# Letting the whole program, and not only its tails, issue in emission order on TensorE, VectorE and ScalarE

## The chip, the cores and the metric

The kernel runs on one core of one Trainium2 chip. A core has TensorE (PE in the profile: matmuls; PEld: its weight loads), VectorE (DVE), ScalarE (ACT), GpSimd (POOL) and SyncE (SP, here only issuing transfers), each with its own queue of instructions that it runs in the order in which they stand. The metric is the device time in microseconds (us) of the whole program; lower is better.

## The reference

Two layers of an encoder on 256 tokens of width 2048, float32, with sizes of all weights in the hundreds of megabytes. Each layer has an attention part and a feed-forward part, each between two norms that a conditioning vector `c` modulates:

```python
cond = jax.nn.silu(c)
for layer in range(2):
    mod = cond @ ada_w[layer] + ada_b[layer]            # 2048 x 12288
    sh1, sc1, g1, sh2, sc2, g2 = split(mod, 6)
    h = rms_norm(x, norm_g[layer, 0]) * (1 + sc1) + sh1
    y = local_dilated_mixer(...) if layer == 0 else diff_attention(...)
    x = x + g1 * rms_norm(y, norm_g[layer, 1])
    h = rms_norm(x, norm_g[layer, 2]) * (1 + sc2) + sh2
    y = conv_ffn(...)                                   # 2048 -> 2 x 5504 -> 2048, a width-3 convolution, gelu
    x = x + g2 * rms_norm(y, norm_g[layer, 3])
```

## The kernel before

All weights stream through the core once. `Plan.order` writes one sequence of 512 KB units: weight units, and between them units of the modulation matrix `ada_w` (a kernel-wide name: "modulation units"). SP fetches them in this sequence into a ring of nine tiles `raw` (`prefetch`, `load`): the next fetch is issued when the tile it writes has been used up.

A weight unit is split into a high and a low part so that TensorE multiplies at full rate and nearly full precision: ScalarE copies `raw` to `whi` (L259), VectorE subtracts to get `wlo` (L309, in `lows`), each from a ring of four. TensorE runs three products a tile (high x high, high x low, low x high): L655, L657, L658 in `feat_units` (feature-major, 256 columns) and L622 to L624 in `mm_tok` (token-major, 512). A modulation unit is multiplied by its entry of `silu(c)` and added to an accumulator `aacc` by VectorE: L280, L296 or L305 for the first of a chunk of sixteen, L284 for the others; for a few, the product is made on TensorE as rows (L272). When a chunk is complete, `ada_finish` sums `aacc` over the partitions with eight matmuls (L459; with rows also L462) and `columns` (L471, L474 on VectorE) writes the scales and shifts `mod`.

`Affine` applies them to the transposed, normalised rows (L509 on ScalarE, L511 on VectorE), `high` (L514) and `low` (L518) split the result into `hT`, which the matmuls read. The transposed rows come from `chunk_T`: scale on ScalarE (L529), four transposes on TensorE (L523), copy on ScalarE (L537). It runs eight times at the start and eight times in `late_tail`, from `Norm.keep`.

`Stream.done` is called when a weight unit's matmuls have been written: it frees the unit's place, takes up the next units as far as the split ring reaches (`advance`), runs the stages due of the chains of attention steps (`tick`), and writes the low parts. So the program emits its work already interleaved by hand. Attention 0 goes through the depth in four blocks (`GK`), and the first seven column units of feed-forward 0 in three (`FK`: k 0 to 7, 8 to 11, 12 to 15), since their modulations come late.

What stands in the queues is set in two ways. Inside `with tc.manual_schedule(engines=ORDERED)`, TensorE, VectorE and ScalarE get their instructions in the order in which the program emits them. Everywhere else a scheduler of the tile framework places them by its own model of readiness. Before the change only `tail` stood in such a block:

```python
if late_mods:
    late_tail(acc, ch, skew, run, got, evac, n0, n1)
else:
    with tc.manual_schedule(engines=ORDERED):
        tail(acc, ch, skew, run, got, evac, n0, n1, head or (lambda n: None))
```

`tail` ends feed-forward 0, attention 1 and feed-forward 1; `late_tail` ends attention 0.

Of the kernel before, what the change touches and what calls it, by code (L numbers as in the profile page):

```python
# [39 lines left out]
class Plan:  # L40
    """The order in which weight units and modulation units reach the chip."""

# [45 lines left out]
    def token_chunks(self, w, ks, late=0, lc=2, last=False):  # L88
        """512 columns at a time; of the first lc chunks, the last units come after all others"""
        pairs = [ks[i:i + 2] for i in range(0, len(ks), 2)]  # L90
        head = pairs[:len(pairs) - late]
        order = [(ch, head) for ch in range(lc)] + [(ch, pairs[len(head):]) for ch in range(lc)]
        order += [(ch, pairs) for ch in range(lc, 4)]
        for ch, ps in order:
            n = len(self.units)
            for p in ps:
                self.rows(w, p[0], len(p), ch * 512, 512)
            if last and ch == 3:
                u = len(self.units) - n
                skew = min(u, SPLIT_BUFS + HELD)  # L100
                self.held |= set(range(n + u - skew, n + u - SPLIT_BUFS))
# [49 lines left out]
    def put(self, nw, na, p=1.0):  # L151
        """nw weight units with na modulation units spread among them"""
        e = self.ia + na
        for k in range(nw):
            t = e - na + round(na * ((k + 1) / nw) ** p)
            while self.ia < t:
                self.seq.append(("a", self.ia))
                self.ia += 1
            self.seq.append(("w", self.iw))
            self.iw += 1  # L160
        while self.ia < e:
            self.seq.append(("a", self.ia))
            self.ia += 1
# [25 lines left out]
def encoder_kernel(ctx: ExitStack, tc: tile.TileContext, x, c, ada_w, ada_b, norm_g,  # L189
# [15 lines left out]
    def vy():  # L205
        return cp.tile([P, 2, D], F32, name="vy")

    plan = Plan(ab_w_in, ab_w_out, c_w_in, c_w_out, ffn_w_up, ffn_w_down)
    units, seq = plan.units, plan.seq

    class Stream:
# [100 lines left out]
        def advance(self, limit=None, lows=True, n=None):  # L312
            """use up what has been loaded, as far as the split buffers reach"""
            if n is not None:
# [36 lines left out]
        def open(self, n):  # L351
            """let n of the gated modulation units through"""
            self.gate += n
            self.advance()
# [18 lines left out]
        def chain(self, *stages, delay=0):  # L373
            """stages one tick after another, each given what the one before returned; older chains go first"""
            age = self.age = self.age + 1

            def run(k, v):
                r = stages[k](v)
                if k + 1 < len(stages):
                    self.at(1, lambda: run(k + 1, r), age)  # L380
            self.at(1 + delay, lambda: run(0, None), age)
# [14 lines left out]

# [1 line left out]
    def rows_tile():  # L398
# [37 lines left out]

# [1 line left out]
    def gate_rows(l, m):  # L438
# [36 lines left out]

# [1 line left out]
    def sums():  # L477
# [20 lines left out]
    class Affine:  # L498
        """the modulated rows of feature tiles k.. from src, split into high and low parts"""

# [33 lines left out]
    def chunk_T(t, ch, r, dst):  # L534
        """rows 4 ch.. of the normalised and transposed x"""
        z = normed(t, ch, r, tmp.tile([P, 512], F32, name="hf", bufs=3), True)
# [5 lines left out]
    class Norm:  # L542
        """x += gate * rms_norm(y), then the modulated rms_norm of x, transposed and split, for one token block"""

# [69 lines left out]

# [1 line left out]
    def mm_tok(dst, act, kt, t, hi, lo, first, last):  # L616
# [9 lines left out]
    def tok_units(dsts, act, ks, first=True, last=True, one_bank=False):  # L626
        """dsts[t] += act block t times the next weights, rows ks"""
        n = 0
        while n < len(ks):
            i, (hi, lo) = st.take()  # L630
            a = hi.shape[1]
# [7 lines left out]
    def feat_units(acc, k0, kn, n):  # L639
        """one bank: acc[:, j] += (next weights).T @ h for n // 128 feature tiles"""  # L640
        hT = cur["hT"]
# [23 lines left out]

# [1 line left out]
    def feat_out(pool, acc, scale, name, bufs=1):  # L667
# [17 lines left out]
    def probs_T(pool, parts):  # L685
        """the transposed probabilities: parts[t] lists what is summed, each with its normalising diagonal"""
        pt = bank().rearrange("p (k q) -> p k q", k=2)
# [174 lines left out]

# [1 line left out]
    def out_chunks(act, ks, evac, late=0, lc=2, norms=None, late_mods=False, head=None):  # L864
# [252 lines left out]

# [1 line left out]
    v_acc, v_got = [], []  # L1119
# [199 lines left out]
```

## Time and profile before

| what | value |
|---|---|
| device time, median of 3 runs | 2326.72 us (2321.35 to 2329.6) |
| span of the profiled execution | 2334.3 us |
| TensorE busy | 2226.5 us, 95% |
| VectorE / ScalarE / GpSimd busy | 1620.0 (69%) / 1055.0 (45%) / 45.5 us (2%) |
| transfers | 587.14 MB, mean 252 GB/s |
| mean granted TensorE clock | 0.980 |

The profiled execution has its span and no time of its own beside it; the span is 7.6 us over the median of the runs, inside 0.4%. In a profile line the idle time before an instruction stands in brackets with what ended it. The granted clock of TensorE (a share of full speed) falls to one half after a time without much work on it. A stage without loss has TensorE busy for all of its length.

The program's stages in this execution, read from the lines that run in them: start and attention 0's k-blocks up to 180 us, the rest of attention 0 to 330, `late_tail` to 370, feed-forward 0's k-blocks to 440, feed-forward 0 to 1180, attention 1 to 1600, feed-forward 1 to the end.

### The profile page before, as it was taken

Reading aid. Unit: us, or ns where it says so; the run is one execution under the profiler, and the core shown is the slowest. Engines: PE = TensorE matmul, PEld = TensorE weight load, DVE = VectorE, ACT = ScalarE, POOL = GpSimd, SP = SyncE. Lnnn points to the kernel's source line nnn. Section 1 sums busy time; section 2 is a strip of 40 time slices with the busy share of each in tenths; the row PEclk is TensorE's granted clock in tenths of the full one; section 3 lists DMA queues with packets and bytes.
Section 4 is the critical chain, followed back from the end, with each engine's and each line's share of the span. In section 5 each row is a group of like instructions: output and inputs, shape, how many; then the busy total and the mean of one; then the engine's idle time right before and its main releaser. Section 6 shows DMA issues by size and latency. Waiting matters only on the chain.

```text
span 2334.3 us, 37324 instructions
## 1 busy us (share of the span) xinstructions
PE 2226.5 (95%) x14961; PEld 2030.9 (87%) x14961; DVE 1620.0 (69%) x1802; ACT 1055.0 (45%) x1451; POOL 45.5 (2%) x72
## 2 busy tenths in 40 slices
PE   5689999999999999999999999999999999999998
PEld 3679978999877999987888999888999988999986
DVE  7888987887666677776687886657565545565555
ACT  4334455544333334434554554446444444444443
POOL 0000000000000000000000110000000000000000
PEclk8889999999999999999999999999999999999999
DMA  9999989898778888887589996665677666666652
GB/s 343 367 329 318 327 292 316 294 306 287 249 263 273 277 268 270 273 261 265 177 287 334 308 307 212 212 198 162 200 205 203 199 206 207 193 205 201 178 187 104
DMA packets 390427, 587.14 MB, mean 252 GB/s; under 512 B 18110, under 2 KB 256360, under 8 KB 389612
## 3 DMA queue, kind: packets, MB, share of 16 engines
q1 hardware_dynamic: 390252, 584.75, 77.3%
q8 instruction: 117, 1.92, 0.3%
q14 instruction: 58, 0.48, 0.1%
HBM read 582.58 MB, written 2.10 MB: 250 GB/s over the span
## 4 chain that ended last, share of the span: by engine, by line
PE 58%; DMA 17%; issue 13%; DVE 10%; ACT 1%; POOL 1%; DVEq 0%; POOLq 0%; ACTq 0%
DMA raw<-in_ada_w_dram 14%; PE bank L657 11%; PE bank L655 11%; PE bank L658 11%; PE bank L623 7%; PE bank L622 7%; PE bank L624 7%; DVE wlo L309 4%; DVE aacc L284 4%; DMA raw<-in_ffn_w_down_dram 2%; DMA raw<-in_ffn_w_up_dram 1%; PE bank L459 1%; DMA raw<-in_ab_w_in_dram 1%; PE bank L794 1%; PE bank L523 1%
## 5 line engine op out<-in xcount | busy, mean ns | idle before, releaser
L259 ACT ACTIVATE whi<-raw 128x1024 fp32r<-128x1024 f32 x708 | 740.5, 1053 | 873.9 <-PE bank L657 399.6
L309 DVE TENSOR_TENSOR wlo<-raw,whi 128x1024 fp32r<-128x1024 f32 x708 | 856.9, 1217 | 369.3 <-ACT whi L259 356.6
L658 PE MATMUL bank<-hT,wlo 128*128 128x256 f32 x3616 | 1022.7, 283 | 20.1 <-DVE wlo L309 20.0
L655 PE MATMUL bank<-hT,whi 128*128 128x256 f32 x3616 | 1027.9, 284 | 0.0
L657 PE MATMUL bank<-hT,whi 128*128 128x256 f32 x3616 | 1018.8, 282 | 0.2 <-DVE hT L518 0.2
L658 PEld LDWEIGHTS bank<-hT,wlo 128*128 128x128 f32 x3616 | 685.9, 190 | 26.8 <-DVE wlo L309 26.1
L655 PEld LDWEIGHTS bank<-hT,whi 128*128 128x128 f32 x3616 | 686.4, 190 | 3.1 <-ACT whi L259 1.0
L657 PEld LDWEIGHTS bank<-hT,whi 128*128 128x128 f32 x3616 | 686.1, 190 | 3.2 <-issue 1.7
L284 DVE SCALAR_TENSOR_TENSOR aacc<-raw,ccol,aacc 128x1024 f32<-128x1024 f32 x352 | 454.1, 1290 | 209.3 <-DMA raw<-in_ada_w_dram 207.0
L623 PE MATMUL bank<-wlo,act 128*128 128x512 f32 x656 | 261.5, 399 | 12.7 <-DVE wlo L309 12.7
L622 PE MATMUL bank<-whi,act 128*128 128x512 f32 x656 | 259.8, 396 | 0.0
L624 PE MATMUL bank<-whi,act 128*128 128x512 f32 x656 | 259.6, 396 | 0.0
L623 PEld LDWEIGHTS bank<-wlo,act 128*128 128x128 f32 x656 | 123.8, 189 | 48.6 <-DVE wlo L309 20.4
L622 PEld LDWEIGHTS bank<-whi,act 128*128 128x128 f32 x656 | 123.9, 189 | 29.0
L624 PEld LDWEIGHTS bank<-whi,act 128*128 128x128 f32 x656 | 123.9, 189 | 28.5
L622 PE MATMUL bank<-whi,hT 128*128 128x512 f32 (+1 forms) x192 | 76.0, 400 | 14.6 <-ACT hT L514 14.6
L1046 ACT ACTIVATE cv<-cv 128x512 f32<-128x512 f32 (+1 forms) x44 | 27.4, 622 | 106.0 <-DVE cv L1042 105.8
L623 PE MATMUL bank<-wlo,hT 128*128 128x512 f32 (+1 forms) x192 | 75.1, 393 | 0.0
L624 PE MATMUL bank<-whi,hT 128*128 128x512 f32 (+1 forms) x192 | 72.2, 385 | 0.0
L622 PE MATMUL bank<-whi,oT 128*128 128x512 f32 x176 | 71.0, 403 | 0.0
L623 PE MATMUL bank<-wlo,oT 128*128 128x512 f32 x176 | 69.6, 396 | 0.0
L624 PE MATMUL bank<-whi,oT 128*128 128x512 f32 x176 | 69.4, 395 | 0.0
(168 smaller groups left out, 1381.5 us busy)
## 6 DMA issues: line engine op xcount, KB each, us to landing
raw<-in_ada_w_dram SPq DMA_DIRECT2D x384, 512.0 KB, 5.3
raw<-in_ffn_w_up_dram SPq DMA_DIRECT2D x344, 512.0 KB, 4.7
raw<-in_ffn_w_down_dram SPq DMA_DIRECT2D x168, 512.0 KB, 5.2
raw<-in_c_w_in_dram SPq DMA_DIRECT2D x96, 512.0 KB, 5.3
raw<-in_ab_w_in_dram SPq DMA_DIRECT2D x56, 512.0 KB, 6.2
raw<-in_c_w_out_dram SPq DMA_DIRECT2D x32, 512.0 KB, 5.0
raw<-in_ab_w_out_dram SPq DMA_DIRECT2D x16, 512.0 KB, 5.6
gb<-in_norm_g_dram SPq DMA_DIRECT2D x3, 1024.0 KB, 4.8
```

Of the source, the lines that this page charges most:

```text
L259: nc.scalar.activation(hi, v, AF.Copy)
L284: nc.vector.scalar_tensor_tensor(self.acc, t, col, self.acc, op0=ALU.mult, op1=ALU.add)
L309: nc.vector.tensor_tensor(lo, v, hi.bitcast(F32), op=ALU.subtract)
L459: nc.tensor.matmul(t[:, j:j + 1], acc[:, j * P:(j + 1) * P], ones[:, 0:1], start=True, stop=rows is None)
L523: nc.tensor.transpose(ps[:, q * P:(q + 1) * P], src[:, q * P:(q + 1) * P], ident)
L622: nc.tensor.matmul(dst, ah, hi, start=first, stop=False, skip_group_check=True)
L623: nc.tensor.matmul(dst, ah, lo, start=False, stop=False, skip_group_check=True)
L624: nc.tensor.matmul(dst, al, hi, start=False, stop=last, skip_group_check=True)
L655: nc.tensor.matmul(acc[:, j], wh, hT[:, k, 0], start=k == 0 and j == 0, stop=False, skip_group_check=True)
L657: nc.tensor.matmul(acc[:, j], wh, hT[:, k, 1], start=False, stop=False, skip_group_check=True)
L658: nc.tensor.matmul(acc[:, j], wl, hT[:, k, 0], start=False, stop=k == KT - 1, skip_group_check=True)
L1046: nc.scalar.activation(cv[:, :nj], cv[:, :nj], AF.Gelu_apprx_tanh)
```

## The change

One line opens the manual schedule at the head of the kernel, so that it holds to the end. The inner block around `tail` stays and changes nothing more. Everything else in the difference is comments taken out, which moves all later lines by one: L284 before is L285 after.

```diff
     def vy():
         return cp.tile([P, 2, D], F32, name="vy")

+    ctx.enter_context(tc.manual_schedule(engines=ORDERED))
     plan = Plan(ab_w_in, ab_w_out, c_w_in, c_w_out, ffn_w_up, ffn_w_down)
```

SP and GpSimd are not in `ORDERED`. GpSimd's order is the same; SP's fetches of units keep their sequence, and a few small loads (convolution weights, `c_lambda`, a 1 MB row of `norm_g`) stand earlier or later among them. The inside of the three `tail` calls is unchanged, and on all three engines the order now is emission order throughout. Three places follow; numbers behind names are those of buffers, and the change shifts them by two (`raw_8197` before is `raw_8199` after).

VectorE in feed-forward 0, around the modulation unit in `raw_8197`. Before:

```order
L284 SCALAR_TENSOR_TENSOR aacc_8099<-raw_8132,ccol_67,aacc_8099 128x1024
L309 TENSOR_TENSOR wlo_8130<-raw_7921,whi_8129 128x1024
L309 TENSOR_TENSOR wlo_8164<-raw_7955,whi_8163 128x1024
L284 SCALAR_TENSOR_TENSOR aacc_8099<-raw_8197,ccol_67,aacc_8099 128x1024
L309 TENSOR_TENSOR wlo_8195<-raw_7988,whi_8194 128x1024
L309 TENSOR_TENSOR wlo_8229<-raw_8026,whi_8228 128x1024
```

After:

```order
L310 TENSOR_TENSOR wlo_8197<-raw_7990,whi_8196 128x1024
L1061 TENSOR_TENSOR act_7295<-cv_7959,act_7295 128x2x256
L310 TENSOR_TENSOR wlo_8231<-raw_8028,whi_8230 128x1024
L285 SCALAR_TENSOR_TENSOR aacc_8101<-raw_8099,ccol_69,aacc_8101 128x1024
L310 TENSOR_TENSOR wlo_8265<-raw_8058,whi_8264 128x1024
...
L285 SCALAR_TENSOR_TENSOR aacc_8101<-raw_8134,ccol_69,aacc_8101 128x1024
L310 TENSOR_TENSOR wlo_8302<-raw_8104,whi_8301 128x1024
L310 TENSOR_TENSOR wlo_8336<-raw_8138,whi_8335 128x1024
L285 SCALAR_TENSOR_TENSOR aacc_8101<-raw_8199,ccol_69,aacc_8101 128x1024
```

The modulation product stood ahead of the low part made from `raw_7988`; now that low part (`wlo_8197`) and four later ones come first.

ScalarE in `late_tail`: `hf` and `vy` are the two ScalarE steps of `chunk_T`, the `junk` rows the squares of token block 1 for its norm. Before:

```order
L529 ACTIVATE hf_3179<-xs_75,rs_r_3138 128x512
L491 ACTIVATE junk_3151,ssq_3148<-xs_75 128x512
L491 ACTIVATE junk_3154,ssq_3148<-xs_75 128x512
L537 ACTIVATE vy_2935<-bank_3165 128x512
L491 ACTIVATE junk_3157,ssq_3148<-xs_75 128x512
L537 ACTIVATE vy_2935<-bank_3173 128x512
L491 ACTIVATE junk_3160,ssq_3148<-xs_75 128x512
L537 ACTIVATE vy_2935<-bank_3181 128x512
L529 ACTIVATE hf_3187<-xs_75,rs_r_3138 128x512
L529 ACTIVATE hf_3199<-xs_75,rs_r_3197 128x512
```

After:

```order
L492 ACTIVATE junk_3153,ssq_3150<-xs_77 128x512
L492 ACTIVATE junk_3156,ssq_3150<-xs_77 128x512
L492 ACTIVATE junk_3159,ssq_3150<-xs_77 128x512
L492 ACTIVATE junk_3162,ssq_3150<-xs_77 128x512
L530 ACTIVATE hf_3165<-xs_77,rs_r_3140 128x512
L538 ACTIVATE vy_2937<-bank_3167 128x512
L530 ACTIVATE hf_3173<-xs_77,rs_r_3140 128x512
L538 ACTIVATE vy_2937<-bank_3175 128x512
L530 ACTIVATE hf_3181<-xs_77,rs_r_3140 128x512
L538 ACTIVATE vy_2937<-bank_3183 128x512
```

All four squares now come first, and each scaling is followed by the copy of its own transpose. The eight chunks at the start read the same way. On TensorE, the row products (L272) of three modulation units, which stood between the transposes, now follow the last one, with three more that already did.

VectorE at attention 0's second k-block: `aacc_381` is the chunk whose columns (`mod`) the block needs, `aacc_514` the next one. Before:

```order
L284 SCALAR_TENSOR_TENSOR aacc_381<-raw_425,ccol_67,aacc_381 128x1024
L471 TENSOR_TENSOR mod0_338<-bank_572,abc_69 128x4
L280 TENSOR_SCALAR aacc_514<-raw_430,ccol_67 128x1024
L471 TENSOR_TENSOR mod1_340<-bank_572,abc_69 128x4
L474 SCALAR_TENSOR_TENSOR mod1_340<-mod1_340,ngc_70 128x4
L284 SCALAR_TENSOR_TENSOR aacc_514<-raw_434,ccol_67,aacc_514 128x1024
L284 SCALAR_TENSOR_TENSOR aacc_514<-raw_437,ccol_67,aacc_514 128x1024
L518 TENSOR_TENSOR hT_166<-hf_620,hT_166 128x4x128
```

After:

```order
L285 SCALAR_TENSOR_TENSOR aacc_383<-raw_427,ccol_69,aacc_383 128x1024
L281 TENSOR_SCALAR aacc_516<-raw_432,ccol_69 128x1024
L285 SCALAR_TENSOR_TENSOR aacc_516<-raw_436,ccol_69,aacc_516 128x1024
L285 SCALAR_TENSOR_TENSOR aacc_516<-raw_439,ccol_69,aacc_516 128x1024
...
L310 TENSOR_TENSOR wlo_560<-raw_508,whi_559 128x1024
L285 SCALAR_TENSOR_TENSOR aacc_516<-raw_514,ccol_69,aacc_516 128x1024
L285 SCALAR_TENSOR_TENSOR aacc_516<-raw_518,ccol_69,aacc_516 128x1024
L472 TENSOR_TENSOR mod0_340<-bank_574,abc_71 128x4
L472 TENSOR_TENSOR mod1_342<-bank_574,abc_71 128x4
L475 SCALAR_TENSOR_TENSOR mod1_342<-mod1_342,ngc_72 128x4
```

Ten instructions of the next chunk now stand ahead of the columns. The third block reads the same; the fourth has three. In feed-forward 0's k-blocks the Affine of k 8 to 11 moves back 31 to 37 places, behind the columns of the chunk for k 12 to 15 and the five VectorE steps that compute `lambda`.

## The prediction, as it was put on record

> **What bounds the kernel now.** I read the page first, then time windows cut at the program's stages, then the waits and timelines of the stages that were not full. The page:
>
> ```profile
> span 2334.3 us, 37324 instructions
> PE 2226.5 (95%) x14961; PEld 2030.9 (87%) x14961; DVE 1620.0 (69%) x1802; ACT 1055.0 (45%) x1451; POOL 45.5 (2%) x72
> PE 58%; DMA 17%; issue 13%; DVE 10%; ACT 1%; POOL 1%; DVEq 0%; POOLq 0%; ACTq 0%
> ...
> raw<-in_ada_w_dram SPq DMA_DIRECT2D x384, 512.0 KB, 5.3
> ```
>
> TensorE is busy for 95% of the span, yet the chain that ended last is only 58% TensorE: 17% of it runs over transfers and 10% over VectorE. So the order on VectorE can matter. The last row is for later: a modulation tile of 512 KB lands 5.3 us after its issue. The windows (columns: stretch, length, busy us of each engine with its count, granted clock, DMA share, GB/s) say where:
>
> ```profile
> 0.00:50.00 50.00, 22.73 (x66) 14.24 (x67) 35.20 (x51) 25.65 (x52) 4.91 (x22) 0.88 0.97 352
> 50.00:100.00 50.00, 39.05 (x242) 35.29 (x241) 45.66 (x43) 16.50 (x22) 0.00 (x0) 0.88 1.01 351
> 100.00:150.00 50.00, 30.46 (x174) 27.47 (x174) 42.95 (x41) 16.93 (x28) 3.79 (x2) 0.77 1.00 352
> 180.00:330.00 150.00, 150.00 (x1050) 139.58 (x1049) 136.87 (x171) 72.09 (x123) 0.00 (x0) 1.00 0.94 321
> 330.00:370.00 40.00, 39.33 (x160) 23.57 (x158) 26.95 (x42) 28.00 (x58) 3.35 (x8) 0.95 0.83 273
> 370.00:440.00 70.00, 68.85 (x554) 68.49 (x555) 55.63 (x65) 28.85 (x37) 3.79 (x2) 0.96 0.92 299
> 440.00:560.00 120.00, 120.00 (x1000) 119.04 (x1000) 103.12 (x116) 60.10 (x73) 0.00 (x0) 1.00 0.92 305
> 560.00:1100.00 540.00, 513.60 (x3454) 466.48 (x3453) 368.83 (x374) 212.93 (x245) 0.00 (x0) 0.99 0.83 268
> 1600.00:2334.00 734.00, 724.92 (x5130) 677.20 (x5129) 414.67 (x443) 326.79 (x374) 1.10 (x2) 1.00 0.64 191
> ```
>
> Three regimes: up to 150 us transfers set the pace (share 1.0), with VectorE next (35.2, 45.7, 43.0 of 50 us); 180 to 330 and 440 to 560 are full on TensorE; 560 to 1100 leaves TensorE 26.4 us idle although the transfers are less busy than before (0.83). After 1600 only the drain at the end is idle.
>
> **The gain: 560 to 1100 us.** The waits from 600 to 1100 (us in total, times, longest):
>
> ```profile
> DVE aacc L284 <- DMA raw<-in_ada_w_dram: 143.2, 75, 4.3
> PEld bank L623 <- DVE wlo L309: 20.4, 19, 2.2
> PEld bank L658 <- DVE wlo L309: 17.7, 20, 3.0
> PE bank L658 <- DVE wlo L309: 13.5, 18, 2.8
> PE bank L623 <- DVE wlo L309: 12.7, 16, 1.8
> ```
>
> and the same first line for 440 to 560 us:
>
> ```profile
> DVE aacc L284 <- DMA raw<-in_ada_w_dram: 3.8, 3, 2.7
> ```
>
> One such case in the timeline (start, us, engine, line):
>
> ```profile
> 863.43 1.28 DVE L284 SCALAR_TENSOR_TENSOR aacc<-raw,ccol,aacc 128x1024 f32<-128x1024 f32 x1 [3.62 <-DMA raw<-in_ada_w_dram]
> 864.63 2.35 DVE L309 TENSOR_TENSOR wlo<-raw,whi 128x1024 fp32r<-128x1024 f32 x2
> 865.91 0.39 PE L658 MATMUL bank<-hT,wlo 128*128 128x256 f32 x1 [1.10 <-DVE wlo L309]
> 866.13 0.28 PE L655 MATMUL bank<-hT,whi 128*128 128x256 f32 x1
> 866.25 0.28 PE L657 MATMUL bank<-hT,whi 128*128 128x256 f32 x1
> ```
>
> VectorE stands 3.62 us before a modulation product (L284) whose weights have not landed; behind it wait two low parts (L309), and TensorE waits for the first. The scheduler put these products 7 to 9 places ahead of where the program emits them. From 440 to 560 the same mix stands almost in emission order, and TensorE is full at 305 GB/s. What is to be had: 540 − 513.6 = 26.4 us idle; each of the 73 waits also hides 0.28 − 0.12 = 0.16 us, since a matmul is listed with 0.28 us but follows at 0.12: 11.7; clock 0.99 over 540 us adds some 3. Together 41. Emission order puts the low parts first, so I take −41. The product's own wait, if any, then stands behind the low parts. Bounds 30 to 44 (0 in the third rival).
>
> **The cost at the start (0 to 165 us).** `chunk_T` (L529, a transpose, L537) is emitted strictly alternating; the scheduler had run the next L529 under the transpose:
>
> ```profile
> 24.94 0.19 ACT L491 ACTIVATION_READ_ACCUMULATOR junk<-xs 128x1 f32 x1
> 30.24 0.71 ACT L529 ACTIVATE hf<-xs,rs_r 128x512 f32<-128x512 f32 x1
> 32.17 0.59 ACT L537 ACTIVATE vy<-bank 128x512 f32<-128x512 f32 x1
> 34.92 0.59 ACT L537 ACTIVATE vy<-bank 128x512 f32<-128x512 f32 x1
> 76.23 0.16 DVE L471 TENSOR_TENSOR mod<-bank,abc 128x4 f32<-128x4 f32 x1 [3.73 <-PE bank L459]
> 76.31 0.74 DVE L280 TENSOR_SCALAR aacc<-raw,ccol 128x1024 f32<-128x1024 f32 x1
> ```
>
> From an L529 to its own L537 are 1.93 us (30.24 to 32.17), plus about 0.5 to the next: 2.45. Eight from 25.1 end at 44.7 instead of 35.5: +9.2 for the weight splits behind, whose low parts stand ahead of the last two products. Then the columns of a block (L471, L474) release its Affine and its matmuls. Before, they ran at 76.23, ahead of ten instructions of the next chunk. Now those stand in front: eight products of 1.3, one L280 of 0.74, one low part of 1.2 are 12.3 us, less the 3.73 that VectorE idled: 8.5 us, at the second and again at the third block. The most is 9.2 + 17 = 26; the least 9, if all that work only comes forward from the next block. I take 17, between them: the products are indeed needed soon after, but with a DMA share of 1.00 a full ring of raw tiles means transfers lost. The Trainium skill's "Perfetto Trace Analysis", Roofline, lets one core's 16 DMA engines reach about 435 GB/s; by that the transfers could catch up, 83 GB/s over 352, and an estimate of this term would be 9 instead of 17. The rows side against it: three windows at 351 to 352 with share 0.97 to 1.01.
>
> **The layer-0 tail (`late_tail`, 330 to 400 us).**
>
> ```profile
> 344.89 1.95 ACT L529 ACTIVATE hf<-xs,rs_r 128x512 f32<-128x512 f32 x3
> 350.53 0.20 ACT L491 ACTIVATION_READ_ACCUMULATOR junk<-xs 128x1 f32 x1
> 357.03 1.08 ACT L537 ACTIVATE vy<-bank 128x512 f32<-128x512 f32 x2 [0.47 <-PE bank L523]
> 354.52 1.88 PE L272 MATMUL bank<-raw,cdiag 128*8 128x512 f32 x4
> 362.60 0.38 PE L459 MATMUL bank<-ones,aacc 128*128 128x1 f32 x2
> 370.39 0.58 PE L655 MATMUL bank<-hT,whi 128*128 128x256 f32 x1
> ```
>
> Before, three L529 of block t=0 ran at 344.89, ahead of the squares of t=1, which end at 350.7. Now the squares come first, then eight chunks one at a time: 350.7 + 8 × 2.45 = 370.3, against 358.1. On TensorE six pairs of row products (L272, some 1.8 us a pair, by 354.52) stand here, three of them in gaps between transposes; now all six follow the last transpose: about 10.6 us from 369.7, so 380.3. The 16 column products took 362.6 to 370.4; now 388.1. Columns, Affine and high part add 1.5: the up projection starts at about 389.6, not 370.4. I take +19. The least is 9 (chunks at 2.1 us with the clock up, row products again in the gaps); the most 25 (the held raw tiles also delay their queue).
>
> **The first feed-forward units by k (`FK`, 400 to 445 us).**
>
> ```profile
> 375.46 0.33 DVE L511 TENSOR_SCALAR hf<-vy,mod,mod 128x128 f32<-128x128 f32 x1
> 423.92 0.23 DVE L471 TENSOR_TENSOR mod<-bank,abc 128x4 f32<-128x4 f32 x2 [7.22 <-PE bank L459]
> 430.35 0.68 DVE L518 TENSOR_TENSOR hT<-hf,hT 128x512 fp32r<-128x512 f32 x1
> ```
>
> The Affine of k 8 to 11 ran from 375 us on, 31 to 37 places ahead; its matmuls began at 412 without a stall. Emitted, it stands behind the columns of the next chunk (423.92) and the lambda's five small steps. TensorE then waits for columns, steps, Affine (4 × 0.33), high and low parts, and again at k 12 to 15, where 423.92 to 431.0 shows the chain taking 7.1 us with other work between. Two stalls of 7 to 10 us would be 17, less what TensorE waits already (1.2 in 370 to 440), plus half clock after each, up to 5. I take +20; bounds 5 (data early enough) and 28. On the clock: 330 to 370 was granted 0.95 and 370 to 440 0.96, so 2.0 + 2.8 = 4.8 us of clock were lost on 1.8 us idle (0.67 + 1.15): low activity, not only idleness, costs clock. The Trainium skill's "TensorE: Matmul & The Clock Gate", Part 1, has one busy window of about 3.4 us restore full speed; an estimate by it is 1.7 us a stall, 3.4 for two, and the term would be 18 or 19.
>
> **Smaller.** Matmuls that ran early under an attention step or a norm now wait in line:
>
> ```profile
> PE bank L822 <- DVE smc L815: 4.6, 5, 2.3
> ```
>
> This row (1100 to 1600 us) prices it: 0.9 us a turn for the eight heads' transposes; I take +3, +3 where the second feed-forward starts, and +3 where the first one's tail hands over to the value heads, less 3 for modulation waits between 1200 and 1600: +6 (bounds −3 and +12). Attention 0 (180 to 330) moves by two places at most under full TensorE, and after 1600 the order hardly changes: 0. SP's and POOL's own issue costs nothing.
>
> **Sum.** 17 + 19 + 20 + 6 − 41 = +21 on 2334.3: 2355. That execution lies 7.6 us over the median of the runs, 2326.72, so 2348.
>
> **Rivals.**
> 1. Faster: lateness in layer 0 does not add up. If each late block's products are work already done for the next, and transfers go on meanwhile, the terms fall to 9 + 9 + 5 + 3 = 26, under the 41: −15, 2312. It decides once layer 0's losses stay below 41. For it: VectorE is 83% busy in the first 150 us, not full, and the three terms were bounded apart. Against: share 1.00 until 150 us leaves nothing to catch up with.
> 2. No change: losses of about 41, or a gain that shrinks with them: 2327. For it: the low half of my bounds; against: all three terms would have to be short.
> 3. The gain is not there. A product run nine places later frees its raw tile some 10 us later; nine tiles of 0.52 MB at 290 GB/s (268 × 540/500) turn round in 16.3 us, and 5.3 of that is the transfer, 11 left. If that is short, TensorE waits for weights instead: +62, 2388. For it: 10 against 11. Against: 440 to 560 holds 305 GB/s in this very order with a full TensorE.
>
> **Chances and range.** Forecast (2334 to 2362) 0.60; rival 1 0.19; no change 0.12; rival 3 0.09. Of this kernel 0.3% (7 us) can be told from no change; so faster 0.20, same 0.13, slower 0.67. From 2316 to 2374 about 0.1 is left out at either end.
>
> **What the next profile would show.** Right: 560 to 1100's work with TensorE over 99% and L284's wait for data near zero; L537 alternating with L529 at 2.2 to 2.5 us; attention 0's four k-blocks starting some 10, 20, 25 and 17 us later; the up projection at about 407 (389.6 and the start's 17); two idle gaps of 7 us or more in the k-blocks. Wrong: block starts that move by under 5 us, or L309 waiting on data between 600 and 1100.

## The result and the profile after

The changed kernel takes 2395.29 us (median of 4 runs, 2393.02 to 2397.23) against 2328.16 us for the kernel before (2321.35 to 2330.22): ratio 1.0298, 95% interval 1.0282 to 1.0314. It is slower, as forecast, but by 67 us instead of 21, and outside the range given. In the profiled execution the span grew from 2334.3 to 2392.0 us.

The page of the changed kernel:

```profile
span 2392.0 us, 37423 instructions
PE 2241.2 (94%) x14961; PEld 2045.9 (86%) x14961; DVE 1634.8 (68%) x1802; ACT 1061.1 (44%) x1452; POOL 50.0 (2%) x72
...
PE 78%; issue 11%; DVE 6%; ACT 3%; DMA 1%; POOL 1%; SPq 0%; DVEq 0%; POOLq 0%; ACTq 0%
```

Transfers have all but left the chain that ended last, 17% before and 1% now, and VectorE went from 10% to 6%; TensorE's share rose from 58% to 78%. Yet the span is 58 us longer. The windows show where, cut at the stages, which come later here (the first three at the same times as before):

```profile
0.00:50.00 50.00, 17.46 (x45) 9.16 (x46) 30.49 (x42) 23.10 (x42) 4.90 (x22) 1.00 0.85 303
50.00:100.00 50.00, 32.47 (x152) 29.43 (x152) 41.53 (x41) 14.16 (x22) 0.00 (x0) 0.85 0.88 310
100.00:150.00 50.00, 36.15 (x178) 32.70 (x179) 37.09 (x35) 15.95 (x25) 1.90 (x1) 0.71 0.95 329
200.00:350.00 150.00, 145.62 (x1044) 135.77 (x1043) 129.10 (x161) 68.33 (x114) 0.00 (x0) 1.00 0.90 304
350.00:420.00 70.00, 55.40 (x209) 34.27 (x207) 39.78 (x48) 30.39 (x58) 4.29 (x8) 0.83 0.76 253
420.00:500.00 80.00, 65.64 (x508) 64.62 (x509) 50.72 (x62) 29.30 (x39) 3.79 (x2) 0.85 0.69 225
620.00:1160.00 540.00, 540.00 (x3696) 499.27 (x3696) 402.11 (x401) 235.54 (x266) 0.00 (x0) 1.00 0.88 287
1250.00:1660.00 410.00, 382.96 (x2435) 343.44 (x2435) 297.88 (x355) 195.78 (x337) 28.30 (x28) 0.98 0.74 247
```

The seventh line is the gain: TensorE 540.00 of 540 us busy, 3696 matmuls where the window of before held 3454. All the others lose: at the start the share of the transfers fell from 0.97 to 1.01 before to 0.85 to 0.95, and TensorE stands idle 15 us in 350 to 420, 14 us in 420 to 500 and 27 us in attention 1. The window of attention 1 before has 11 us idle:

```profile
1200.00:1600.00 400.00, 388.80 (x2470) 350.20 (x2470) 297.97 (x351) 196.41 (x333) 24.92 (x28) 0.98 0.78 259
```

How much each stage is worth is read best by following the same matmul through two traces. The table gives how much later TensorE starts the same matmuls than in the kernel before (median within 6 us of a point of the trace of before), as differences between the ends of stages. For the kernel before stands a second profile of it, taken with the experiments (span 2319.6 us), since the first turned out to be unusual in one stage (last experiment). A stage that runs as before shows 0.

```
us lost (+) or won (-)   start  attn 0  late   k-     ffn 0  hand-  attn 1  attn 1's  ffn 1's  rest
by stage                               tail   blocks        over   heads   end       start
before, first profile     -0.5    0.0    1.4    2.2   10.6    0.2    0.4     3.2      -0.4   -2.3
before, third profile      1.2    0.0    1.3    0.3    0.0   -0.5   -0.2     2.1      -1.5   -2.3
changed kernel            25.7    7.2   25.5   20.3  -30.4    2.7   18.3     1.6       4.1   -2.3
e1_ffn0                    0.3    0.1   -0.1    1.4  -30.2    0.1    0.3    -0.4      -1.8   -2.3
e2_dve                    11.4    0.4    6.9   18.4  -30.4    0.1    4.0    -1.7       0.7    0.5
e8_nodve                  15.3    1.5   22.0   19.5   -0.4    7.4   12.5     4.5       4.9   -2.2
e3_pipe                   16.2    5.7   20.3   20.7  -30.5    3.9   19.7     1.6       4.1   -2.3
e4_gap                    25.6    5.6   24.9   20.6  -30.5    4.2   -0.3    -1.4       4.7   -2.3
e5_mend                   12.9   12.1   19.5   17.1  -30.4    3.9    0.0    -2.9       4.6    0.5
e7_early                  17.0    7.2   20.8   13.3  -30.4    4.1   -0.4    -1.5       5.2    0.1
e9_spread                 25.9    7.2   20.3   20.6  -30.5    3.7   18.5     1.6       4.1   -2.3
e10_keep                  16.4    7.2   22.4   20.6  -30.4    3.8   19.6     1.6       4.6    0.1
e6_two                    -0.6    0.0    1.3    1.4  -30.2    0.5   -0.2    -2.9      -1.8   -2.2
```

The row of the changed kernel adds up to 72.7 us; the spans differ by 72.4. That is 5 us more than by the medians, since the execution of the second profile took 2321.39 us, 4 us under the median of its runs. Differences of 2 to 3 us between rows are also found between the two other profiles of before.

### The profile page after: what moved, and what is told of

It is laid out like the page before. It is cut to its first block, busy times and chain, and to the rows that moved or that the text cites. A ratio compares the mean times of both kernels' runs of the same rounds, so it can differ in the third digit from the quotient of the medians.

```text
span 2392.0 us, 37423 instructions
## 1 busy us (share of the span) xinstructions
PE 2241.2 (94%) x14961; PEld 2045.9 (86%) x14961; DVE 1634.8 (68%) x1802; ACT 1061.1 (44%) x1452; POOL 50.0 (2%) x72
## 4 chain that ended last, share of the span: by engine, by line
PE 78%; issue 11%; DVE 6%; ACT 3%; DMA 1%; POOL 1%; SPq 0%; DVEq 0%; POOLq 0%; ACTq 0%
PE bank L658 15%; PE bank L656 15%; PE bank L659 15%; PE bank L625 9%; PE bank L623 9%; PE bank L624 9%; DVE aacc L285 2%; DVE wlo L310 1%; PE bank L524 1%; PE bank L460 1%; POOL rs_r L487 1%; ACT junk L492 1%; PE bank L795 1%; PE bank L832 1%; ACT whi L260 0%
## 5 line engine op out<-in xcount | busy, mean ns | idle before, releaser
L285 DVE SCALAR_TENSOR_TENSOR aacc<-raw,ccol,aacc 128x1024 f32<-128x1024 f32 x352 | 451.9, 1284 | 11.4 <-DMA raw<-in_ada_w_dram 9.8
L623 PE MATMUL bank<-whi,hT 128*128 128x512 f32 (+1 forms) x192 | 79.1, 412 | 25.4 <-ACT hT L515 25.4
L625 PE MATMUL bank<-whi,hT 128*128 128x512 f32 (+1 forms) x192 | 78.6, 409 | 2.3 <-DVE hT L519 2.3
L487 POOL TENSOR_TENSOR rs_r<-rs_m,mhalf 128x1 f32<-128x1 f32 x32 | 31.1, 978 | 1963.5 <-DVE rs_m L485 1963.5
```

What stands on the lines that cost most here:

```text
L285: nc.vector.scalar_tensor_tensor(self.acc, t, col, self.acc, op0=ALU.mult, op1=ALU.add)
L487: nc.gpsimd.tensor_tensor(r, m, mhalf, op=ALU.pow)
L623: nc.tensor.matmul(dst, ah, hi, start=first, stop=False, skip_group_check=True)
L625: nc.tensor.matmul(dst, al, hi, start=False, stop=last, skip_group_check=True)
```

## The experiments

### Only feed-forward 0 in emission order

```diff
+            if l == 0 and part == 0:
+                man.enter_context(tc.manual_schedule(engines=ORDERED))
             for j in range(p // 2 * 2, fn, 2):
...
                        (lambda: [next_norm(...) ...]) if final else None, head=head)
+        man.close()
```

> The manual schedule is opened only in layer 0's feed-forward, behind its three k-blocks, and closed at that feed-forward's end; all else stands as the scheduler placed it before. Theory A (the gain and the losses lie in different stretches and don't depend on each other): the 41 us that the changed kernel won back between 600 and 1160 us come whole and nothing else is lost: 2328 - 41 = 2287 us. Rival B (the gain in the changed kernel came only because TensorE ran late there, so that the transfers had a lead of some 75 us to land in): with TensorE on time the modulation tiles land as late as before and at most a third comes, 2310 to 2328 us.

2291.08 us against 2324.44, ratio 0.9855 (0.9835 to 0.9875). The gain of the changed kernel came whole with TensorE on time, 30.2 us by the table and 33 by the runs; 41 it was only against the first profile. The window of that stretch and its longest waits:

```profile
560.00:1060.00 500.00, 500.00 (x3451) 463.90 (x3450) 377.54 (x377) 217.63 (x245) 0.00 (x0) 1.00 0.88 290
```

```profile
ACT whi L259 <- PE bank L657: 139.6, 87, 3.6
DVE wlo L309 <- ACT whi L259: 113.5, 146, 2.5
```

TensorE is full for 500 us. VectorE's wait for a modulation tile, at the head of the list before, is not among the waits any more. ScalarE now waits for a place in the ring of split tiles, which TensorE frees as it goes, and VectorE for ScalarE. Gain and losses are separate.

### VectorE alone, and all but VectorE

```diff
+    ctx.enter_context(tc.manual_schedule(engines={ENG.DVE}))                    # e2_dve
+    ctx.enter_context(tc.manual_schedule(engines={ENG.PE, ENG.Activation}))     # e8_nodve
```

> Only VectorE issues in emission order throughout; TensorE and ScalarE are placed by the scheduler. Theory A (the losses in the k-blocks and the gain are VectorE's order; the losses of chunk_T and of attention 1's transposes are ScalarE's and TensorE's): the start loses 15 to 20 instead of 26, the late tail some 10 instead of 25, the first feed-forward k-blocks 15 to 19, attention 1 under 5 instead of 18, the gain stays 41: 2328 + 18 + 10 + 17 + 4 - 41 = 2336 us. Rival B (TensorE's and ScalarE's order do not matter, VectorE's does it all): as the changed kernel, 2395 us.

> The complement of the run with VectorE alone: TensorE and ScalarE in emission order throughout, VectorE placed by the scheduler. Theory A (the engines' shares add up to the changed kernel's): gain 0 between 600 and 1100; start 26 - 10 = 16, late tail 25 - 5 = 20, k-blocks 18 - 17 = 1, attention 1 about 18 if its waits are TensorE's order: 2324 + 16 + 20 + 1 + 6 + 18 = 2385 us. Rival B (the losses need VectorE's order too, since TensorE in emission order waits only where VectorE is late): start under 10, late tail under 15, attention 1 under 6: 2355 us or less.

2331.45 us (ratio 1.0022, 1.001 to 1.0034) and 2406.87 us (1.036, 1.0339 to 1.038). VectorE's order alone brings the whole gain, 30.4, and without it there is none, 0.4. The first run came out 5 us under its expectation: its start lost 11.4 where 15 to 20 had been expected, and its gain is 30.4 instead of 41. Without VectorE's order the wait for modulation tiles stands as before (580 to 1150 us):

```profile
DVE aacc L286 <- DMA raw<-in_ada_w_dram: 147.8, 92, 3.5
```

At the start and in the late tail the two shares add up roughly, 11.4 + 15.3 to 25.7 and 6.9 + 22.0 to 25.5, so theory A held there. In the k-blocks they don't: 18.4 and 19.5 to 20.3. Either order alone is enough to delay the Affine chain. That stage (19.5 instead of 1) is most of the 22 us by which the second run exceeds its expectation. Attention 1's loss comes mostly with TensorE's and ScalarE's order (12.5 against 4.0): there TensorE waits 8.5 us in all at the transposes of the heads, in seven waits, and with VectorE's order alone not at all.

### chunk_T one step ahead

```diff
-                chunk_T(t, ch, rs[t], zT[...])
+                z1 = chunk_N(t, ch, rs[t])          # scaling and transposes
+                if z is not None:
+                    chunk_C(*z)                     # the copy of the chunk before
+                z = (z1, zT[...])
```

> The changed kernel with chunk_T emitted one step ahead: the next chunk's scaling and transposes stand before the copy of the last one, at the start and in late_tail. Theory A (the alternation of scaling, transpose and copy costs what it lengthens): the eight chunks end 8 to 9 us earlier at the start and as much in the late tail, 2395 - 17 = 2378 us. Rival B (the k-blocks are bound by the columns that stand behind the next chunk and by split buffers that TensorE holds, so an earlier start is absorbed in the next wait): under 5 us in all, 2390 us or more.

2378.72 us (ratio 1.0225, 1.02 to 1.025), close to the 2378 expected. By the table 9.5 us are won at the start, as theory A had it, but only 5.2 in the late tail, where 8 to 9 had been expected. In the changed kernel the eight chunks at the start read, first and last:

```profile
24.42 0.70 ACT L530 ACTIVATE hf<-xs,rs_r 128x512 f32<-128x512 f32 x1
26.33 0.60 ACT L538 ACTIVATE vy<-bank 128x512 f32<-128x512 f32 x1 [1.21 <-PE bank L524]
26.82 0.71 ACT L530 ACTIVATE hf<-xs,rs_r 128x512 f32<-128x512 f32 x1
...
43.22 0.60 ACT L538 ACTIVATE vy<-bank 128x512 f32<-128x512 f32 x1 [1.21 <-PE bank L524]
```

2.40 us a chunk (24.42 to 26.82), 1.21 of it ScalarE waiting for the transpose; they end at 43.8 instead of 35.5.

### A stage between norm and turn in attention 1

```diff
-        st.chain(scores, soft, expo, norm, turn, apply, rstd, scaled, back, finish)
+        st.chain(scores, soft, expo, norm, lambda _: None, turn, apply, rstd, scaled, back, finish)
```

> The changed kernel with one empty stage between norm and turn in attention 1's heads, so that the transposes of the probabilities are emitted one weight unit later. Theory A (TensorE stands at the transposes only because VectorE's normalising steps, queued behind products and low parts, are not done when it gets there): the waits at the transposes go and attention 1 loses 2 to 4 us instead of 18, 2395 - 15 = 2380 us. Rival B (VectorE is late by more than one unit's 3 us, or the delay moves to the next stage): 2390 us or more.

2371.57 us (ratio 1.0194, 1.0171 to 1.0217), 8 us under theory A's 2380: attention 1's 18.3 us became −0.3, where 2 to 4 had been left. One head in the changed kernel, ScalarE with the last exponential, then VectorE, then TensorE:

```profile
1365.36 0.19 ACT L807 ACTIVATION_READ_ACCUMULATOR smc<-smc,nm 128x1 f32 x1
```

```profile
1364.33 1.28 DVE L285 SCALAR_TENSOR_TENSOR aacc<-raw,ccol,aacc 128x1024 f32<-128x1024 f32 x1
1365.53 1.22 DVE L310 TENSOR_TENSOR wlo<-raw,whi 128x1024 fp32r<-128x1024 f32 x1
1366.66 1.28 DVE L285 SCALAR_TENSOR_TENSOR aacc<-raw,ccol,aacc 128x1024 f32<-128x1024 f32 x1
1367.86 1.22 DVE L310 TENSOR_TENSOR wlo<-raw,whi 128x1024 fp32r<-128x1024 f32 x1
...
1370.63 0.48 DVE L816 SCALAR_TENSOR_TENSOR smc<-smc,rden 128x256 f32<-128x256 f32 x1
```

```profile
1367.03 0.28 PE L659 MATMUL bank<-hT,wlo 128*128 128x256 f32 x1
1370.48 0.41 PE L823 MATMUL bank<-ident,smc 128*128 128x128 f32 x2 [3.17 <-DVE smc L816]
1371.17 0.44 PE L823 MATMUL bank<-ident,smc 128*128 128x128 f32 x2 [0.28 <-DVE smc L816]
...
1372.42 0.41 PE L656 MATMUL bank<-hT,whi 128*128 128x256 f32 x1
1372.63 0.41 PE L658 MATMUL bank<-hT,whi 128*128 128x256 f32 x1
```

The same head before:

```profile
1323.38 0.19 ACT L806 ACTIVATION_READ_ACCUMULATOR smc<-smc,nm 128x1 f32 x1
1328.26 0.87 DVE L815 SCALAR_TENSOR_TENSOR smc<-smc,rden 128x256 f32<-128x256 f32 x2
1328.31 0.28 PE L658 MATMUL bank<-hT,wlo 128*128 128x256 f32 x1
1328.88 0.41 PE L822 MATMUL bank<-ident,smc 128*128 128x128 f32 x2 [0.29 <-DVE smc L815]
```

From the last exponential to the last normalising step VectorE takes 5.6 us in both kernels (1365.55 to 1371.11 and 1323.57 to 1329.13), with products and low parts in front of these steps in both. What differs is TensorE's list. Before, the scheduler put matmuls of the next unit in front of the transposes: 41 matmuls start between the exponential and the transposes, and TensorE waits 0.29 us. Now there are 13, and TensorE stands for 3.2 us. The matmuls behind are then listed with 0.41 us at a pace of 0.21 instead of 0.28 at 0.12: the granted clock is 0.50 from 1371.8 to 1375.2. Five of the eight heads wait, the first four 2.5, 3.5, 1.8 and 3.4 us and the last 2.6. In those four VectorE takes 5.6 to 6.0 us, against 5.6 to 8.7 before, and 13 to 27 matmuls stand in front of the transposes, against 41 to 55. The waits of the first four in the changed kernel (1300 to 1480 us), and what is left of them with the stage:

```profile
PE bank L823 <- DVE smc L816: 11.1, 8, 3.2
```

```profile
PE bank L823 <- DVE smc L816: 0.6, 2, 0.3
```

### The program's order mended at five places

On top of the two edits above: the same empty stage in attention 0's first kind of head, the columns of the next k-block ahead of the next chunk, and the second k-block's Affine ahead of the flush.

```diff
             st.advance(plan.mark[q])
             st.flush()
+            st.cap = plan.mark[q + 1] if q + 1 < len(plan.mark) else None   # advance() stops there
...
-                    st.flush()
+                if n > 1:
+                    st.flush()
                 for k in range(k0, k1, 4):
                     ...
+                if n == 1:
+                    st.flush()
...
-        st.chain(scores, soft, expo, lambda _: diags(norm(None)),
+        st.chain(scores, soft, expo, lambda _: diags(norm(None)), lambda d: d,
```

> The changed kernel, all of it in emission order, with the program's own order mended at five places: chunk_T one step ahead; an empty stage in attention 1's heads (norm to turn) and in attention 0's first kind (normalising to probabilities); in attention 0's k-blocks no unit behind the next mark is taken up before the columns are written; in feed-forward 0's second k-block the Affine is emitted ahead of the flush that writes the columns for k 12 to 15. Theory A (each loss is one misplaced emission): start 26 -> 5 to 10, attention 0's end 6 -> 1, late tail 25 -> 18, k-blocks 18 -> 9, attention 1 18 -> 0 with 9 won at its end; 2324 + 8 + 1 + 18 + 9 + 3 - 9 + 5 - 41 = 2318 us, range 2305 to 2330. Rival B (holding the next chunk back at the marks leaves transfers without a free raw tile, and the start loses by it what the columns win): start stays at 15 or more, 2328 us or more.

2359.87 us (ratio 1.0163, 1.0135 to 1.0191), far from 2318: theory A failed in three of five places. The start lost 12.9 where 5 to 10 had been expected, only 3.3 less than with `chunk_T` ahead alone (`e3_pipe`, 16.2). With the empty stage attention 0 lost 12.1 instead of 5.7 to 7.2, more and not less. The Affine ahead of the flush won 3.6 of 20.7.

When the columns (L474 before) of attention 0's four k-blocks are written says more about the start, in us later than in the second profile of before:

```
                 1st    2nd    3rd    4th    whole start
changed kernel   8.3   21.0   25.7   18.8    25.7
e3_pipe         -0.9   11.7   16.0    9.1    16.2
e5_mend         -0.1    4.0    7.3   10.8    12.9
```

Holding the next chunk back brings the columns of the second and third block 7.7 and 8.7 us forward, close to the 8.5 a block at which the ten instructions in front of them had been priced. But what is held back has to be done before the fourth block, whose columns come 1.7 us later than without the hold. So the start gains little, as rival B had it; whether transfers without a free tile are the reason, as it said, the run doesn't show.

The changed kernel loses 6.9 us more behind the columns of the fourth block (18.8 to 25.7). Its rows there, VectorE and then ScalarE:

```profile
163.20 1.60 DVE L475 SCALAR_TENSOR_TENSOR mod<-mod,ngc 128x4 f32<-128x4 f32 x1
```

```profile
167.43 1.06 ACT L260 ACTIVATE whi<-raw 128x1024 fp32r<-128x1024 f32 x1 [8.99 <-PE bank L658]
168.39 1.63 ACT L510 ACTIVATE hf<-vy,mod,mod 128x128 f32<-128x128 f32 x4
```

The Affine (L510) starts 3.6 us after the end of that last step of the columns, because a weight split that waits for TensorE stands ahead of it on ScalarE. The step itself takes 1.6 us instead of 0.16, for a reason that was not followed up. In the kernel before, the Affine starts right behind the step (143.73 and 143.69 us). In `e5_mend`, which takes no unit up ahead of the columns, the Affine follows as soon as they are written, and only 2.1 us are lost behind the fourth block's columns.

### The second k-block's Affine inside the first

```diff
+                if n != 1:
+                    rows_in(k0, k1)
+                if n == 0:
+                    st.at(3, lambda: rows_in(FK[1], FK[2]))
```

> The changed kernel, all in emission order, with chunk_T one step ahead, the empty stage between norm and turn in attention 1, and the Affine of feed-forward 0's k 8 to 11 emitted three units into the first k-block instead of at its end. Theory A (at a k-block's edge TensorE waits for the Affine chain of some 8 us only because nothing is emitted between; early emission hides it, as the scheduler did): the k-blocks lose 9 instead of 18, and with 17 from chunk_T and 24 from attention 1 the time is 2395 - 17 - 24 - 9 = 2345 us. Rival B (the early Affine waits for its columns and holds up the low parts behind it on VectorE): 2354 us or more.

2351.23 us (ratio 1.0119, 1.0099 to 1.0139), between theory A's 2345 and rival B's 2354; it holds the two edits on `chunk_T` and attention 1 as well. The k-blocks lose 13.3 instead of 20.7, 7.4 of the 9 expected. In the changed kernel an edge between blocks reads:

```profile
476.23 1.11 DVE L512 TENSOR_SCALAR hf<-vy,mod,mod 128x128 f32<-128x128 f32 x4
478.04 0.69 DVE L519 TENSOR_TENSOR hT<-hf,hT 128x512 fp32r<-128x512 f32 x1 [0.69 <-ACT hT L515]
480.24 0.69 DVE L519 TENSOR_TENSOR hT<-hf,hT 128x512 fp32r<-128x512 f32 x1 [1.51 <-ACT hT L515]
```

The chain of scale, high and low for two token blocks takes 4.7 us, with nothing else between. TensorE waits for it three times in 420 to 530 us, 5.5 us at the end of the late tail and 7.1 and 6.2 us at the two edges:

```profile
PE bank L656 <- ACT hT L515: 18.7, 3, 7.1
```

### The late tail

```diff
-        n0.keep()
-        st.open(gates.pop(0))
+        n0.keep(lambda: st.open(1))      # e9: one gated unit behind each chunk; the same for n1.keep
```

> The changed kernel with late_tail's last gates opened one by one behind each of its eight chunks, so that the row products of six modulation units stand between the transposes again. Theory A (those row products, some 10 us, are serial behind the last transpose): the late tail loses 15 to 17 instead of 25, 2395 - 9 = 2386 us. Rival B (a row product of 1.7 us between two chunks delays the next transpose by as much, since the chunks alternate between ScalarE and TensorE): 2393 us or more.

2389.19 us (ratio 1.0265, 1.0214 to 1.0315): the late tail lost 20.3 instead of 25.5, some half of what theory A gave. Moving the four chunks of token block 0 ahead of block 1's squares, with `chunk_T` a step ahead:

> The changed kernel with chunk_T one step ahead, and in late_tail the four chunks of token block 0 emitted ahead of the squares of block 1. Theory A (the chunks of block 0 waited behind squares that wait for TensorE's last outputs): the late tail loses 13 to 15 instead of 25 (19 with chunk_T ahead alone), 2378 - 5 = 2373 us. Rival B (VectorE's residual sums of block 1, now behind the start of the chunks, end as late as before and the second half of the chunks with them): 2377 us or more.

2386.22 us (ratio 1.0252, 1.0202 to 1.0301), a late tail of 22.4 where `chunk_T` ahead alone left 20.3: rival B held, the move wins nothing. The late tail of the changed kernel, ScalarE and TensorE:

```profile
384.94 0.71 ACT L530 ACTIVATE hf<-xs,rs_r 128x512 f32<-128x512 f32 x1
...
403.73 0.60 ACT L538 ACTIVATE vy<-bank 128x512 f32<-128x512 f32 x1 [1.20 <-PE bank L524]
```

```profile
402.58 1.11 PE L524 MATMUL bank<-ident,hf 128*128 128x128 f32 x4 [1.30 <-ACT hf L530]
403.62 11.56 PE L273 MATMUL bank<-raw,cdiag 128*8 128x512 f32 x24
426.68 0.58 PE L656 MATMUL bank<-hT,whi 128*128 128x256 f32 x1 [5.49 <-ACT hT L515]
```

The chain is the one forecast: eight chunks of 2.41 us, then 11.6 us of row products, the columns, the Affine. Why neither run won all that was expected is not shown.

### Two stretches in emission order

Feed-forward 0 as in the first run, and attention 1's heads to its end with the empty stage.

```diff
+        man.enter_context(tc.manual_schedule(engines=ORDERED))
         for h in range(8):
...
         out_proj(oT, list(range(KT)), 1, f_head)
+        man.close()
```

> Before, with the manual schedule in two stretches: layer 0's feed-forward behind its k-blocks, and attention 1 from its first head to its end, with the empty stage between norm and turn. Theory A (the stretches don't depend on each other, and attention 1 in emission order with the stage wins the 9 us seen at its end): 2291 - 9 = 2282 us. Rival B (those 9 us came from time that TensorE lost earlier in that attention, or from the 37 us by which everything ran late): 2288 to 2293 us.

2288.43 us against 2323.03, ratio 0.9855 (0.9827 to 0.9883), not to be told from the first run (rival B). By the table attention 1 wins 3.1 us against 0.1 in the first run; part of the 9 us comes from reading against the first profile, in which that attention's end runs 3.2 us late. These two are the best seen, 1.45% under the kernel before.

### The kernel before, profiled again

No edit.

> The kernel before, unchanged, profiled once more. Its first profiled execution spans 2334.3 us, some 10 us over the median of its runs, and the changed kernels' gains by trace (41 to 49 us) are larger than by the runs (33 to 35). Theory A (the excess lies in feed-forward 0, where VectorE waits for tiles that have only just landed, so that small delays of transfers are paid in full): this execution spans some 2324 us and TensorE is idle some 18 instead of 26 us there. Rival B (the excess lies elsewhere, at the start): the gain there stays 41.

> The kernel before, unchanged, profiled a third time: as the run beside it. Theory A: a span within 5 us of 2324, with its differences to the first profile in feed-forward 0. Rival B: differences at the start.

2325.56 and 2325.23 us, ratios 0.9998 (0.9977 to 1.0019) and 1.0 (0.9986 to 1.0015), with spans of 2319.6 and 2320.0 us. Theory A held. In the second profile feed-forward 0 reads

```profile
560.00:1100.00 540.00, 521.41 (x3487) 471.11 (x3486) 374.66 (x379) 219.78 (x253) 0.00 (x0) 1.00 0.83 271
```

```profile
DVE aacc L284 <- DMA raw<-in_ada_w_dram: 146.8, 86, 3.7
...
PEld bank L623 <- DVE wlo L309: 18.8, 23, 1.5
PEld bank L658 <- DVE wlo L309: 12.9, 20, 1.5
```

18.6 us idle on TensorE instead of 26.4, and its longest wait for a low part 1.5 us instead of 3.0, though VectorE waits as often and almost as long. Of the 14.7 us between the two spans, 10.6 lie in this stage. What made the first execution slower there is not shown: its modulation tiles landed a median 4.5 us after their issue in this window, against 4.7 and 4.6 us in the other two. The third profile agrees with the second there to 0.1 us.

## Why the prediction was wrong

Forecast against measured, by the table (us):

```
term          forecast   bounds      measured
gain             -41     -44 to -30    -30.4
start             17       9 to 26      25.7
late tail         19       9 to 25      25.5
k-blocks          20       5 to 28      20.3
smaller            6      -3 to 12      33.9   (7.2 + 2.7 + 18.3 + 1.6 + 4.1)
rest               0                    -2.3
sum               21                    72.7   (67 by the medians)
```

**Smaller: the step that failed most.** The price of a transpose's wait, 0.9 us from five waits of before, was that of a wait which the scheduler had already cut short by putting matmuls in front. Eight waits at that price are 7.4 us, and the 4.6 us that stood there already would leave the 3 that were taken. Without these matmuls the first four heads lose 4.6 us each (18.3 / 4), 2.8 of it waiting and most of the rest, as far as the head shown tells, the slow pace behind. VectorE did not get later: in the head shown it takes 5.6 us in both kernels from the exponential to the last normalising step. The term had to be worked out from these 5.6 us and from the matmuls that are left to fill them, 13 instead of 41 there; `e4_gap` shows that it is this wait. At attention 0 the same was overlooked because instructions move by two places at most. The trace of the changed kernel has TensorE waiting there for `diag` (2.9 us in two waits); a stage more made it worse, and where all of the 7.2 us come from is not settled.

**Gain: mis-sized by 10.6.** The mechanism was right: VectorE's order alone brings it, in that stretch alone, and the third rival (tiles held too long) is refuted by a full TensorE at 290 GB/s in `e1_ffn0`. The size was that of one execution. It was worked out right for that execution, whose matmuls the changed kernel beats by 41.0 us there. But it ran 10.6 us slower in this stage than two others of the same kernel. The profile's 7.6 us over the median were noted and taken off at the end; that they might lie in the very stage whose stalls were being counted was not asked.

**Start: mis-sized by 8.7.** The alternation cost what was worked out (9.2; `e3_pipe` wins 9.5). The blocks moved as forecast too: "10, 20, 25 and 17" by the signs of the prediction, 8.3, 21.0, 25.7 and 18.8 by their columns, so that part is indeed won back before the fourth block. The sum stopped there, at 17. It left out what comes behind the fourth block's columns, 6.9 us, where a weight split now stands ahead of the Affine. The transfers caught nothing up over these 150 us: they averaged 303 to 329 GB/s here, against 351 to 352 before. The estimate by the Trainium skill's "Perfetto Trace Analysis", Roofline, 9 us, was further off than the 17 by the rows.

**Late tail: mis-sized by 6.5**, just over its upper bound; against the first profile, from which the 19 was worked out, the stage lost 24.1. The steps were right: squares first, chunks of 2.41 for 2.45 us, row products behind. Row products took 11.6 for 10.6 us, and from their end at 415.2 to the first matmul at 426.7 were 11.5 us instead of 9.3. The rest is not followed up.

**k-blocks: right**, by the wait forecast, with some luck in the number: the two waits are 7.1 and 6.2 us, 13.2 together, where 17 had been taken. Behind the first TensorE is busy for 4.0 us at a granted clock of 0.50, behind the second for 6.5 us at 0.51; half of that, about 5.2 us, is lost to the clock, as the 5 us by the rows had it. The 3.4 us by the Trainium skill's "TensorE: Matmul & The Clock Gate", Part 1, were too few here.

Of the forecast's rivals none happened. The measured time lies near the third rival's 2388 by coincidence: the gain came, and the losses were larger. The four lossy terms were each placed inside their bounds as if errors would cancel. Three of the four came out at or above the upper bound, and where the cause was found, in attention 1 and behind the fourth block, it is of one kind: an engine that runs its list in order waits, and nothing is left to fill the time.

## What to carry to other kernels

An order is best kept by hand only where the profile shows the scheduler's to be at fault: one stretch of 500 us gave 1.45%, the whole program cost 3%. Before a scheduler is switched off, list every place where it puts filler ahead of a short dependent chain, however few places it moves. Price the chain by its own length, less the work that is still in front of its reader, never by the wait that is left with the filler in. Here the errors of such terms had one sign and added up. A gain counted in stalls wants a second profile of the same kernel.

## What the runs showed of the hardware

TensorE's clock fell after a stall of 3.2 us and another of 0.3: behind that head's transposes the matmuls went at 0.21 us instead of 0.12, so that 3.5 us of waiting cost about 5 us. The granted clock was 0.50 for 3.4 us there. Over the first four heads of attention 1 the waits at the transposes sum to 11.1 us on TensorE, and the heads lost 18.3.

Two executions of one program, 14.7 us apart in span, differed by 10.6 us in a single stage: the one in which VectorE waits for tiles to land. Its tiles did not land later by the median (4.5 us after issue, against 4.7), so the cause stays open.
